# Local attention's scores of two heads as two 64-row matmuls into two PSUM banks

## The chip, the cores and the metric

One Trainium2 chip; the kernel runs on one of its cores. The core has a matrix engine (TensorE, PE in the profile; its weight loads are PEld), VectorE (DVE), ScalarE (ACT), GpSimd (POOL) and a queue engine (SyncE, SP), with an on-chip memory (SBUF) of 128 partitions and an accumulator memory (PSUM) of eight banks, each 512 float32 wide in every partition. The metric is the time of one execution on the device in microseconds, and a kernel's time is the median of its runs.

## The reference

Two layers over 528 tokens (16 learned ones and 512 of the input), width 1024. In each layer a normalized input is projected and split into three mixers: a state-space mixer (S5), local attention with 8 query heads, 2 key heads and a window of 128, and latent attention with 4 heads over all earlier tokens. The three results are normalized, joined, projected and added to the stream; a squared-ReLU MLP of width 4096 follows. What the change touches is the local attention:

```python
qb = q.reshape(bsz, nb, BLOCK, SWA_KV_HEADS, grp, HEAD_DIM)      # BLOCK 128, 2 key heads, grp 4, HEAD_DIM 64
kk, vv = with_prev(kb), with_prev(vb)                            # a block's keys and the block before
s = jnp.einsum('bnqhgd,bnkhd->bnhgqk', qb, kk) * (HEAD_DIM ** -0.5)
s = s - slopes * dist                                            # and -1e30 outside the window
m = jnp.maximum(jnp.max(s, -1, keepdims=True), sink)
p = jnp.exp(s - m)
p = p / (jnp.sum(p, -1, keepdims=True) + jnp.exp(sink - m))
o = jnp.einsum('bnhgqk,bnkhd->bnqhgd', p, vv)
```

All of it is float32.

## The kernel before

The activations are held transposed, features on partitions. The tokens are cut into two halves, A of 272 and B of 256. The large projections go through `gemm` (L182): a weight block of 1024 x 128 is loaded by SP's queue, split into a high part (ScalarE) and a rest (VectorE, L154), and 24 matmuls with 128 x 128 weights go into one PSUM bank "d", of which there are two. In layer 0, half A, the first nine blocks use the exact float32 weights instead (L174); such a float32 matmul leaves two records in the profile, one a pass.

`weave` sets the order: a main stream (projections, output projection, MLP) yields its estimated time after each block, and two side streams, `s5_half` (the state-space mixer of one half) and `attn_half` (both attentions of one half), are advanced by a given share of it. The tile framework then orders each engine's instructions by priority and by what is ready, gives every tile a buffer of its tag, and makes a new user of a buffer wait until the one before it is released.

PSUM's banks are all in use: "d" has two; "bu" two (one tile); "y", "s", "o" and "pt" one each.

`attn_half` goes over units in three steps that are staggered: `first` computes scores and the softmax of a unit, `second` transposes the probabilities of the unit before (L756, into "pt"), `third` multiplies those of the unit before that with the values (L780, into "o"; two heads side by side, each on 64 of the array's 128 columns). A local unit is one block of 128 queries and two query heads, one of each key head: per layer 8 units for each half, so 32. Its two heads are done by one matmul of 128 rows (L697), since the query tile holds head g on partitions 0 to 63 and head g + 4 on 64 to 127. The keys "k2" are stored twice, once for each key head, with zeros on the other's 64 partitions. The scores of both heads stand side by side in the bank "s", 2 x 256 columns, or 2 x 144 for the first block. The softmax reads each head's part with one fused VectorE instruction (L611); ScalarE's exponentials follow. A unit for the 16 learned tokens (L709) exists in layer 0 only.

In `w_in` block 5 yields the keys: VectorE scales the projection into a scratch tile "ch", and ScalarE copies 64 partitions of it into each key head's part of "k2". The zeros come from GpSimd in `open_layer` (L411).

`s5_half` uses PSUM so: the input is spread over 128 partitions for each of two column blocks (L516, bank "y", copied out by ScalarE), projected to states (L530, "bu", read by VectorE in L535 and L536), scanned, projected back (L574, "y", read in L576), and this twice; then comes a gate (L595, "bu", read in L596) and a column sum for the norm (L224, "y"). `startB` opens half B's projections; in layer 1 its column sums use "y". `s5_prep` builds tables and holds one "y" (L351, L365). In the MLP of layer 1 `gemm` uses "bu" for every second pair of halves (L163).

Of the kernel before, what the change touches and what calls it, by code (L numbers as in the profile page):

```python
# [12 lines left out]
F32 = mybir.dt.float32  # L13
# [7 lines left out]
P = 128  # L21
# [3 lines left out]
NM = 16  # L25
# [51 lines left out]
def hybrid(ctx, tc, xT, wblk, small, wglu, wuq, wukv, bD, cD, ident_d, bias_d, tbias_d, mask_d, rope_d, tau_d, outT):  # L77
# [119 lines left out]
    def chain_tmp():  # L197
        return rows(mk(nt, [P, 3, 272], F32, "ch"))
# [12 lines left out]
    def sumsq(tm, src, nk, n):  # L211
# [7 lines left out]
                V.tensor_tensor(acc, acc, sq, op=ALU.add)  # L219
        return acc  # L220

    def colsum(acc, n, tag, second=None):
        ps = mk(psd if tag == "d" else psm, [P, 512], F32, tag)
        PE.matmul(ps[:, :n], lhsT=ones[:, 0:1].to_broadcast([P, P]), rhs=acc, start=True, stop=second is None)  # L224
        if second is not None:
            PE.matmul(ps[:, :n], lhsT=ones[:96, 0:1].to_broadcast([96, P]), rhs=second, start=False, stop=True)
        return ps[:, :n]
# [34 lines left out]
    def s5_prep(L):  # L262
# [85 lines left out]
        nc.gpsimd.memset(tt, 0.0)  # L348
        nci = vt[:, 0, 1]
        V.tensor_scalar(nci, vt[:, CL - 1, 1], -1.0, None, op0=ALU.mult)  # L350
        t3 = mk(psm, [P, 512], F32, "y")  # L351
        cmul(ws[:, :, :, CL - 1], braw, cr, ci)
        yield 2.4
        for m in range(1, CL):
# [48 lines left out]
    def open_layer(L):  # L403
        kv_ = mk(mem, [P, KVW], F32, "kv")
        L["kh"] = kv_[:96, :4 * T].rearrange("p (d t) -> p d t", d=4)
        L["k2"] = kv_[:, 4 * T:6 * T].rearrange("p (d t) -> p d t", d=2)
        L["vm"] = kv_[:, 6 * T:6 * T + 1280].rearrange("p (t c) -> p t c", t=5)
        L["vs"] = mk(mem, [P, 5, P], F32, "vs")
        for kv in range(2):
            o = 64 * (1 - kv)  # L410
            nc.gpsimd.memset(L["k2"][o:o + 64, kv, :], 0.0)  # L411
        nc.gpsimd.memset(L["vm"][:, 0], 0.0)
        nc.gpsimd.memset(L["vs"][:, 0], 0.0)

    def w_in(L, hf, ar, M):
        l, n, t0 = L["l"], HN[hf], H0[hf]
        a, r = ar

        def scaled(out, ps):
            V.tensor_tensor(out, ps, r[:, :out.shape[1]], op=ALU.mult)  # L420
        M["hf"], M["done"] = hf, set()
        M["y"] = mk(mem, [P, KD, 272], F32, f"big{hf}")
        qq = mk_slot(F32)
        M["q"] = qq[:, 0:1088]
        M["qh"] = qq[:, 1088:2176].rearrange("p (d t) -> p d t", d=4)
        M["u"] = qq[:, 2176:2720].rearrange("p (k t) -> p k t", k=2)
        M["cq"] = qq[:, 2720:3264].rearrange("p (k t) -> p k t", k=2)
        M["ckv"] = qq[:, 3264:3536]
        M["v"] = qq[:, 3536:3808]
        M["rope"] = qq[:, 3808:4352].rearrange("p (k t) -> p k t", k=2)  # L430
        nc.gpsimd.dma_start(out=M["rope"][:, :, :n], in_=rope_d[:, :, t0:t0 + n])
        nc.gpsimd.memset(M["cq"][64:96, 1, :n], 0.0)
        for bi, b in enumerate(ORD[hf]):
            if l + hf == 0 and bi == NF:
                a, _ = gains(l, hf, 0, n, "g_in", False)
            ps, = gemm(l, b, [(a, n)])
            if b < 2:
                V.tensor_tensor(M["u"][:, b, :n].rearrange("p (q k) -> p k q", q=CL),
                                ps[:, :n].rearrange("p (k q) -> p k q", q=CL),
                                r[:, :n].rearrange("p (k q) -> p k q", q=CL), op=ALU.mult)  # L440
            elif b == 2:
                scaled(M["ckv"][:, :n], ps[:, :n])
            elif b == 3:
                t = [x[:, :n] for x in chain_tmp()]
                scaled(t[2], ps[:, :n])
                act(M["cq"][0:64, 1, :n], t[2][0:64])
                V.tensor_tensor(t[0][64:96], t[2][64:96], M["rope"][64:96, 0, :n], op=ALU.mult)
                V.tensor_tensor(t[1][96:128], t[2][96:128], M["rope"][96:128, 1, :n], op=ALU.mult)
                act(t[2][64:96], t[1][96:128])
                V.tensor_tensor(t[0][64:96], t[0][64:96], t[2][64:96], op=ALU.add)  # L450
                act(L["kh"][64:96, :, t0:t0 + n], t[0][64:96].unsqueeze(1).to_broadcast([32, 4, n]))
            elif b == 4:
                scaled(M["cq"][:, 0, :n], ps[:, :n])
            elif b == 5:
                t = chain_tmp()
                scaled(t[0][:, :n], ps[:, :n])
                for kv in range(2):
                    p = slice(64 * kv, 64 * kv + 64)
                    act(L["k2"][p, kv, t0:t0 + n], t[0][p, :n])
            elif b < 10:  # L460
                g = b - 6
                qm = M["q"][:, :1024].rearrange("p (t g c) -> p t g c", t=2, g=4)[:, :, g, :]
                c0 = n - 256
                V.tensor_tensor(qm, ps[:, c0:n].rearrange("p (t c) -> p t c", t=2),
                                r[:, c0:n].rearrange("p (t c) -> p t c", t=2), op=ALU.mult)
                if c0 and l < DEPTH - 1:
                    scaled(M["q"][:, 1024 + NM * g:1024 + NM * g + NM], ps[:, :NM])
            else:
                scaled(M["v"][:, :n], ps[:, :n])
            M["done"].add(b)  # L470
            yield cost(l, hf, FULL_IN, n) if bi < NF or l + hf else cost(l, hf, (), n)
# [8 lines left out]
    def finish(L, M, a0, a1, s5):  # L480
        l, hf = L["l"], M["hf"]
        o0, m = span(l, hf)
        y = M["y"]
        if "mixed" not in M:
            M["mixed"] = mk_slot(F32)[:, :2176].rearrange("p (k t) -> p k t", k=KD) if (l, hf) in FULL_OUT else mk_hl()
        mx_ = M["mixed"]
        tm = mix_tmp(s5)
        acc = sumsq(tm, lambda k: y[:, a0 + k, o0:o0 + m], a1 - a0, m)
        r = rsqrt(tm, colsum(acc, m, "y" if s5 else "o"), m, 128 * (a1 - a0))
        yield 1.5  # L490
        for k in range(a0, a1):
            t = y[:, k, o0:o0 + m]
            if (l, hf) in FULL_OUT:
                V.scalar_tensor_tensor(mx_[:, k, :m], t, sm(l, "g_heads", k), r, op0=ALU.mult, op1=ALU.mult)
                yield 0.4
                continue
            V.tensor_tensor(t, t, r, op=ALU.mult)
            split(mx_[:, 0, k, :m], mx_[:, 1, k, :m], t, sm(l, "g_heads", k))
            yield 0.7

    def s5_half(L, M):
# [7 lines left out]
            s5["sv"] = mk(mem, [P, 2, 8], F32, "sv")  # L509
        sv = s5["sv"]  # L510
        u4 = mk(wk, [P, 2, 272], F32, "u3")
        for o in range(2):
            ups = mk(psm, [P, 512], F32, "y")
            for j in range(4):
                for q in range(CL):
                    PE.matmul(ups[32 * q:32 * q + 32, j * K:j * K + K], lhsT=ident[:, 32 * j:32 * j + 32],  # L516
                              rhs=M["u"][:, o, q * K:q * K + K], start=True, stop=True, tile_position=(0, 32 * q))
            act(u4[:, o, :n], ups[:, :n])
# [6 lines left out]
        for o in range(2):  # L525
# [36 lines left out]
            if hf == 0:  # L562
                V.tensor_tensor(sv[:, 0, iq], wv[:, 0, :, K - 1], qv[:, 1, :, K - 1], op=ALU.subtract)
                V.scalar_tensor_tensor(sv[:, 1, iq], qv[:, 0, :, K - 1], -1.0, wv[:, 1, :, K - 1], op0=ALU.mult, op1=ALU.subtract)
            yps = mk(psm, [P, 512], F32, "y")
            for q in range(CL):
                for m in range(3):
                    for j in range(4):
# [52 lines left out]
    def attn_half(L, M):  # L621
# [68 lines left out]
        def first(u):  # L690
            kind, j, o, g = u
            s_ = mk(wk, [P, 544], F32, "s_", bufs=2)
            if kind == "swa":
                ks, nk = (0, NM + P) if j == 1 else (NM + P * (j - 2), 2 * P)
                sp = score()
                c0 = 512 * ((j - 1) % 2) + P * g
                PE.matmul(sp[:, :2 * nk].rearrange("p (e k) -> p e k", e=2), lhsT=M["q"][:, c0:c0 + P],  # L697
                          rhs=L["k2"][:, :, ks:ks + nk], start=True, stop=True)
                s2 = s_[:, :2 * nk + 2].rearrange("p (e k) -> p e k", e=2)
                ns = L["nsink"]  # L700
                nc.gpsimd.tensor_copy(s2[:, :, nk:], ns[:, :8].rearrange("p (e g) -> p e g", e=2)[:, :, g:g + 1])
                vs = [s2[:, e] for e in range(2)]
                softmax([(vs[e], lambda e=e: [(sp[:, nk * e:nk * e + nk], 0, nk)], bias[:, 4 * e + g, 256 - nk:],
                          ns[:, 4 * e + g:4 * e + g + 1]) for e in range(2)], nk, 0.125, True)
                return vs
            if kind == "swah":
                sp = score()
                for e in range(2):
                    PE.matmul(sp[64 * e:64 * e + 64, :NM], lhsT=M["q"][:, 1024:1088], rhs=L["k2"][:, e, 0:NM],  # L709
                              start=True, stop=True, tile_position=(0, 64 * e))  # L710
                nc.gpsimd.tensor_copy(s_[:, NM:NM + 1], L["nsink"][:, 8:9])
                softmax([(s_, lambda: [(sp[:, :NM], 0, NM)], tbias, L["nsink"][:, 8:9])], NM, 0.125, True)
                return [s_]
# [248 lines left out]
    for l in range(DEPTH):  # L962
# [28 lines left out]

        def s2():
            if not winB:
                startB("y")
            s5_ok = 3
            o = obuf(0)
            tm = [mk(nt, [P, 272], F32, "rl", bufs=2) for _ in range(2)]
# [152 lines left out]
```

## Time and profile before

| | |
|---|---|
| median of 3 runs | 1277.2 us (1275.5 to 1279.62) |
| the profiled execution | 1275.43 us |
| its span, first to last instruction | 1273.5 us |
| mean granted clock of TensorE | 0.986 of full speed |
| TensorE busy | 1214.2 us, 95% |
| VectorE busy | 859.1 us, 67% |
| ScalarE busy | 864.9 us, 68% |
| GpSimd busy | 43.3 us, 3% |

How to read the profile: an engine is busy while one of its instructions runs, and an instruction is named by engine and source line, often with "tile written <- tiles read". A PE form such as 128*64 128x128 is rows and columns of the array that are used, then partitions and columns of the output. Matmuls are pipelined, so the durations of neighbours overlap; the distance from one start to the next tells what an instruction takes in a stream. The chain of waits follows the work that ended last back from the end, at each step to what released it.

### The profile page before, as it was taken

The page shows a single profiled execution, that of the slowest core. Times are in us where ns is not written, and L with a number is a line of the kernel's source. Part 1 is how long each engine was busy: PE and PEld are TensorE (multiplying, and loading weights), DVE is VectorE, ACT ScalarE, POOL GpSimd, SP SyncE. Part 2 cuts the span into 40 slices and gives each one's busy share as a digit, 9 for nine tenths or more (in the row PEclk, how much of TensorE's full clock was granted, in tenths as well). Part 3 has the DMA queues.
Part 4 walks back from the last instruction along what each step waited for, and adds up shares of the span by engine and source line. Part 5 has one row for each costly group of instructions (what it writes and reads, how often), then busy time and mean ns, then how long its engine had stood idle before and what let it go on. Part 6 is the DMA issues. An engine that isn't in the chain of part 4 may idle for free.

```text
span 1273.5 us, 27373 instructions
## 1 busy us (share of the span) xinstructions
PE 1214.2 (95%) x10256; PEld 1131.9 (89%) x10256; DVE 859.1 (67%) x1992; ACT 864.9 (68%) x2012; POOL 43.3 (3%) x103
## 2 busy tenths in 40 slices
PE   6999998999999999899999988999999999999985
PEld 4788886899999999888899987778999999999985
DVE  7888768869755657856776789766684343334775
ACT  6787787997764657766786776798675632534764
POOL 4000002000000000000000000000000000000000
PEclk9999998999999999999999989999989999999998
DMA  6233423254665556433345642324646333334652
GB/s 227 76 100 101 136 66 100 78 166 130 196 181 175 175 175 206 118 123 112 105 150 174 193 141 83 100 76 125 185 145 178 95 96 91 92 101 128 187 185 90
DMA packets 93236, 170.55 MB, mean 134 GB/s; under 512 B 10960, under 2 KB 14032, under 8 KB 93104
## 3 DMA queue, kind: packets, MB, share of 16 engines
q1 hardware_dynamic: 90288, 161.62, 41.7%
q0 software_dynamic: 2816, 7.18, 1.8%
q8 instruction: 81, 1.33, 0.4%
q14 instruction: 51, 0.42, 0.1%
HBM read 166.66 MB, written 2.10 MB: 133 GB/s over the span
## 4 chain that ended last, share of the span: by engine, by line
PE 45%; DVE 4%; ACT 3%; DMA 1%; issue 1%; DVEq 0%; ACTq 0%
PE d L182 32%; PE bu L182 7%; PE o L780 1%; DMA raw<-in_wblk 1%; PE pt L756 1%; PE s L697 1%; DVE big L810 1%; ACT w L133 1%; ACT slot L133 1%; DVE w L154 1%; DVE h L811 1%; PE s L732 1%; ACT ch L133 1%; PE o L224 0%; ACT rl L133 0%
## 5 line engine op out<-in xcount | busy, mean ns | idle before, releaser
L182 PE MATMUL d<-slot,w 128*128 128x256 f32 (+1 forms) x6936 | 911.8, 289 | 20.6 <-ACT slot L133 5.6
L182 PEld LDWEIGHTS d<-slot,w 128*128 128x128 f32 x6936 | 861.7, 190 | 48.9 <-issue 13.9
L154 DVE TENSOR_TENSOR w<-raw,w 128x512 fp32r<-128x512 f32 x578 | 396.9, 691 | 214.3 <-ACT w L133 204.7
L133 ACT ACTIVATE w<-raw 128x512 fp32r<-128x512 f32 x578 | 360.3, 627 | 233.8 <-PE d L182 168.4
L189 DVE TENSOR_TENSOR slot<-rl,slot 128x256 fp32r<-128x256 f32 (+1 forms) x128 | 54.2, 428 | 60.4 <-ACT slot L133 58.2
L182 PE MATMUL bu<-slot,w 128*128 128x256 f32 x768 | 92.9, 280 | 0.0
L182 PEld LDWEIGHTS bu<-slot,w 128*128 128x128 f32 x768 | 91.4, 188 | 0.0
L133 ACT ACTIVATE rl<-d 128x256 f32<-128x256 f32 (+1 forms) x144 | 54.2, 376 | 33.6 <-PE d L182 31.9
L133 ACT ACTIVATE slot<-rl 128x256 fp32r<-128x256 f32 (+1 forms) x128 | 52.6, 419 | 2.6
L133 ACT ACTIVATE rl<-rl 128x256 f32<-128x256 f32 (+1 forms) x128 | 52.6, 418 | 1.9
L174 PE MATMUL d<-slot,raw 128*128 128x272 f32 x144 | 38.5, 413 | 10.6 <-DMA raw<-in_wblk 10.6
L885 DVE TENSOR_TENSOR big<-d,big 128x256 f32<-128x256 f32 (+1 forms) x80 | 34.2, 428 | 15.5 <-PE d L182 12.3
L174 PEld LDWEIGHTS d<-slot,raw 128*128 128x128 f32 x144 | 28.1, 200 | 17.5 <-ACT ch L133 10.6
L133 ACT ACTIVATE ph<-pt 128x512 f32<-128x512 f32 (+2 forms) x66 | 36.4, 552 | 6.4 <-PE pt L756 6.0
L219 DVE TENSOR_TENSOR ch<-ch 128x256 f32<-128x256 f32 (+1 forms) x84 | 35.8, 426 | 5.9 <-ACT ch L133 5.9
L133 ACT ACTIVATE slot<-h,small 128x256 fp32r<-128x256 f32 (+2 forms) x72 | 32.0, 504 | 9.2 <-DVE h L811 4.9
L697 PE MATMUL s<-kv,slot 128*128 128x512 f32 (+1 forms) x64 | 31.5, 574 | 1.5 <-ACT vs L133 0.7
L133 ACT ACTIVATE ch<-h 128x256 f32<-128x256 f32 (+1 forms) x64 | 25.3, 413 | 7.5 <-DVE ch L219 6.6
L192 DVE SCALAR_TENSOR_TENSOR slot<-h,small,slot 128x256 fp32r<-128x256 f32 (+1 forms) x64 | 27.7, 484 | 1.0 <-ACT slot L133 1.0
L732 PE MATMUL s<-kv,slot 96*128 96x264 f32 (+3 forms) x80 | 26.3, 410 | 0.5 <-DVE nm L611 0.4
L780 PE MATMUL o<-ph,vs 128*64 128x128 f32 x256 | 22.7, 286 | 0.0
L810 DVE TENSOR_TENSOR big<-big,ch 128x512 f32<-128x512 f32 (+1 forms) x32 | 21.0, 693 | 0.1
(651 smaller groups left out, 1133.9 us busy)
## 6 DMA issues: line engine op xcount, KB each, us to landing
raw<-in_wblk SPq DMA_DIRECT2D x600, 256.0 KB, 2.7
ph<-in_wuq POOLq DMA_DIRECT2D x8, 256.0 KB, 3.1
h<-in_xT SPq DMA_DIRECT2D x4, 272.0 KB, 4.2
h<-in_xT SPq DMA_DIRECT2D x1, 1024.0 KB, 10.5
ph<-in_wukv POOLq DMA_DIRECT2D x4, 256.0 KB, 3.4
u<-in_wglu POOLq DMA_DIRECT2D x4, 256.0 KB, 3.7
out<-h SPq DMA_DIRECT2D x1, 1024.0 KB, 5.7
out<-h SPq DMA_DIRECT2D x4, 256.0 KB, 2.3
```

Source lines behind the costliest of these rows:

```text
L133: S.activation(out, in_, func, **kw)
L154: V.tensor_tensor(w[:, 1].rearrange("p k m -> p (k m)"), raw, f32(hi), op=ALU.subtract)
L174: PE.matmul(ps[:, :n], lhsT=raw[:, k * P:(k + 1) * P], rhs=a[:, 4 * q + k, :n], start=q + k == 0, stop=q + k == 4)
L182: PE.matmul(ps[:, :n], lhsT=w[:, wi, k, :], rhs=a[:, ai, 4 * q + k, :n], start=i == 0, stop=i == 23)
L189: V.tensor_tensor(lo, src, f32(hi), op=ALU.subtract)
L192: V.scalar_tensor_tensor(lo, src, gain, f32(hi), op0=ALU.mult, op1=ALU.subtract)
L219: V.tensor_tensor(acc, acc, sq, op=ALU.add)
L697: PE.matmul(sp[:, :2 * nk].rearrange("p (e k) -> p e k", e=2), lhsT=M["q"][:, c0:c0 + P], rhs=L["k2"][:, :, ks:ks + nk], start=True, stop= ...
L732: PE.matmul(sp, lhsT=M["qh"][0:96, 2 * g + e, o:o + P], rhs=L["kh"][:, 2 * g + e, c0:c1], start=True, stop=True)
L780: PE.matmul(ops[64 * e:64 * e + 64, :P], lhsT=v, rhs=pp[:, P * e:P * e + P], start=i == 0, stop=i == len(ph) - 1, tile_position=(0, 64 * e))
L810: V.tensor_tensor(x, x, rb, op=ALU.mult)
L885: V.tensor_tensor(ac[:, b, :n], ps[:, :n], ac[:, b, :n], op=ALU.add)
```

## The change

Each head's scores become a matmul of their own on 64 rows: head e uses partitions 64e to 64e + 63 of queries and keys, is put on that row half of the array, and writes to a bank of its own ("s" and a new "s2"). The keys need no zero halves: "kt" holds both key heads on their partitions, and block 5 scales straight into it; scratch tile, copies and the memsets for "k2" go. The learned tokens' unit uses 64 rows and 64 columns for each head. The bank for "s2" is freed by removing "y": its users take a tile of the two banks "bu", the two spreads of `s5_half` one bank of a common tile each, the others the first bank.

```diff
+    def two_banks():
+        return mk(psm, [P, 2, 512], F32, "bu")
+
     def colsum(acc, n, tag, second=None):
-        ps = mk(psd if tag == "d" else psm, [P, 512], F32, tag)
+        ps = two_banks()[:, 0] if tag == "bu" else mk(psd if tag == "d" else psm, [P, 512], F32, tag)
...
-        t3 = mk(psm, [P, 512], F32, "y")
+        t3 = two_banks()[:, 0]
...
-        L["k2"] = kv_[:, 4 * T:6 * T].rearrange("p (d t) -> p d t", d=2)
+        L["kt"] = kv_[:, 4 * T:5 * T]
...
-        for kv in range(2):
-            o = 64 * (1 - kv)
-            nc.gpsimd.memset(L["k2"][o:o + 64, kv, :], 0.0)
...
             elif b == 5:
-                t = chain_tmp()
-                scaled(t[0][:, :n], ps[:, :n])
-                for kv in range(2):
-                    p = slice(64 * kv, 64 * kv + 64)
-                    act(L["k2"][p, kv, t0:t0 + n], t[0][p, :n])
+                scaled(L["kt"][:, t0:t0 + n], ps[:, :n])
...
-        r = rsqrt(tm, colsum(acc, m, "y" if s5 else "o"), m, 128 * (a1 - a0))
+        r = rsqrt(tm, colsum(acc, m, "bu" if s5 else "o"), m, 128 * (a1 - a0))
...
+        both = two_banks()
         for o in range(2):
-            ups = mk(psm, [P, 512], F32, "y")
+            ups = both[:, o]
...
-            yps = mk(psm, [P, 512], F32, "y")
+            yps = two_banks()[:, 0]
...
-                sp = score()
+                sp = [score(), mk(psm, [P, 512], F32, "s2")]
                 c0 = 512 * ((j - 1) % 2) + P * g
-                PE.matmul(sp[:, :2 * nk].rearrange("p (e k) -> p e k", e=2), lhsT=M["q"][:, c0:c0 + P],
-                          rhs=L["k2"][:, :, ks:ks + nk], start=True, stop=True)
+                for e in range(2):
+                    p = slice(64 * e, 64 * e + 64)
+                    PE.matmul(sp[e][:, :nk], lhsT=M["q"][p, c0:c0 + P], rhs=L["kt"][p, ks:ks + nk], start=True, stop=True,
+                              tile_position=(64 * e, 0))
...
-                softmax([(vs[e], lambda e=e: [(sp[:, nk * e:nk * e + nk], 0, nk)], bias[:, 4 * e + g, 256 - nk:],
+                softmax([(vs[e], lambda e=e: [(sp[e][:, :nk], 0, nk)], bias[:, 4 * e + g, 256 - nk:],
...
-                    PE.matmul(sp[64 * e:64 * e + 64, :NM], lhsT=M["q"][:, 1024:1088], rhs=L["k2"][:, e, 0:NM],
-                              start=True, stop=True, tile_position=(0, 64 * e))
+                    p = slice(64 * e, 64 * e + 64)
+                    PE.matmul(sp[p, :NM], lhsT=M["q"][p, 1024:1088], rhs=L["kt"][p, 0:NM],
+                              start=True, stop=True, tile_position=(64 * e, 64 * e))
...
-                startB("y")
+                startB("bu")
```

## Rows read from the trace of the kernel before

**Rows 1.** The page: busy us, share of the span and instructions.
```profile
PE 1214.2 (95%) x10256; PEld 1131.9 (89%) x10256; DVE 859.1 (67%) x1992; ACT 864.9 (68%) x2012; POOL 43.3 (3%) x103
```

**Rows 2.** Stretch, length, busy us of PE, PEld, DVE, ACT, POOL; clock, DMA share, GB/s.
```profile
50.00:75.00 25.00, 23.82 (x144) 17.07 (x143) 20.70 (x88) 23.03 (x71) 2.84 (x8) 1.00 0.32 96
163.00:178.00 15.00, 14.94 (x121) 10.29 (x122) 6.75 (x30) 12.19 (x39) 0.75 (x4) 1.00 0.11 32
569.00:620.00 51.00, 50.39 (x605) 44.53 (x604) 36.78 (x101) 30.98 (x81) 3.27 (x7) 1.00 0.36 109
813.00:840.00 27.00, 26.51 (x180) 19.21 (x178) 18.63 (x62) 25.87 (x74) 1.44 (x6) 1.00 0.17 51
...
770.00:792.00 22.00, 18.50 (x272) 17.03 (x271) 21.70 (x52) 12.81 (x30) 0.00 (x0) 0.92 0.20 60
```

**Rows 3.** The chain of waits near 573 and 822 us: start, us, what.
```profile
572.59 0.86 PE s L697 x2
...
573.99 0.13 PE d L182
574.12 0.40 PE pt L756 x3
...
577.16 0.48 PE s L697 x2
...
821.53 0.59 PE o L780 x8
822.12 1.05 PE s L697 x2
```

**Rows 4.** PE in order of time, 108 to 110 us: start, us, instructions.
```profile
108.09 0.66 PE L780 MATMUL o<-ph,kv 128*64 128x128 f32 x8
108.68 1.10 PE L182 MATMUL d<-slot,w 128*128 128x256 f32 x7
109.71 0.66 PE L780 MATMUL o<-ph,kv 128*64 128x128 f32 x8
```

**Rows 5.** The chain of waits in the MLP of layer 1.
```profile
992.86 5.64 PE bu L182 x48
```

**Rows 6.** PE in order of time: the first and the last of 32 local units.
```profile
50.64 0.75 PE L697 MATMUL s<-kv,slot 128*128 128x288 f32 x2
...
838.48 1.02 PE L697 MATMUL s<-kv,slot 128*128 128x512 f32 x2
```

**Rows 7.** In order of time: state-space halves 1 and 4, by engine.
```profile
98.17 0.49 DVE L576 SCALAR_TENSOR_TENSOR big<-slot,small,y 128x272 f32<-128x272 f32 x1
98.77 0.78 PE L530 MATMUL bu<-u,wt 128*128 128x68 f32 x6
...
771.55 2.00 PE L530 MATMUL bu<-u,wt 128*128 128x64 f32 x16
773.36 2.60 PE L182 MATMUL d<-slot,w 128*128 128x256 f32 x20
779.15 1.01 PE L516 MATMUL y<-slot,ident 128*32 128x64 f32 x32 [3.19 <-DVE slot L438]
...
779.18 0.68 DVE L535 TENSOR_TENSOR wP<-bu,tab 128x512 f32<-128x512 f32 x1
...
780.54 0.37 ACT L133 ACTIVATE u<-y 128x256 f32<-128x256 f32 x1
```

**Rows 8.** Who waited for whom on PE: us in total, times, longest.
```profile
PE d L174 <- DMA raw<-in_wblk: 10.6, 1, 10.6
...
PE y L516 <- ACT u L133: 0.8, 1, 0.8
...
PE s L697 <- DVE nm L611: 0.6, 2, 0.4
```

**Rows 9.** Instructions that write or read tile kv: duration ns, first to last start.
```profile
L133 ACT ACTIVATE kv<-ch x12: 405/428/1112, 27.5 to 800.8; 64x272 f32<-64x272 f32 x4, 64x256 f32<-64x256 f32 x4, 32x1088 f32<-32x1088 f32 x2, 32x1024 f32<-32x1024 f32 x2
L411 POOL MEMSET kv<- x4: 532/534/537, 5.2 to 513.8; 64x528 f32 x4
```

## The prediction

> **What bounds the kernel now.** I read the page first: TensorE (PE) is busy 95% of 1273.5 us, VectorE and ScalarE two thirds [rows 1]. The profiled execution took 1275.43 us, 1.9 more than its span; the median of the runs, 1277.2, stands 0.14% above it. The table by stage then says whether PE is the bound where the change works. The local scores run in four stretches, and PE is busy 95, 99.6, 98.8 and 98.2% of them [rows 2]. In the last of them ScalarE is nearly as full: it has 27 - 25.87 = 1.1 us to spare, and what PE saves beyond that ScalarE holds back. The chain of waits agrees: around 573 and 822 us it runs along PE, through scores (L697), projection matmuls (L182), transposes (L756) and value products (L780) [rows 3].
>
> **The scores, priced.** A float32 matmul leaves two records, one a pass. Of the 32 local units 24 stream 512 columns a pass and 8, those of the first block, stream 288. In the chain a unit of 512 takes 0.86 us between full-array neighbours, 0.43 a pass; one of 288 takes 0.48. Behind a value product (L780), whose matmuls fill half of the array's columns, the same 512 take 1.05 [rows 3]. These 0.2 us are the price of changing how the array is divided, and a second view says so. Eight L780 records from 108.09 us take 0.59 us until the next instruction; the seven L182 behind them take 1.03 until L780 returns [rows 4]. In a long run 48 of L182 take 5.64 us [rows 5], 0.1175 each, so seven are 0.82 and 0.21 is on top. The eight L780 passes of 128 columns would take 0.86 one by one (0.43 x 128/512 = 0.107 each); two at a time they take 0.43, and 0.16 is on top. So column halves run side by side, and each change of division costs 0.16 to 0.21 us: the array runs empty, then the next weights load uncovered.
>
> The Trainium skill (TensorEngine Tiling (Array Packing), Key Properties) says that a switch of the tiling mode drains TensorE, while different tiles work in parallel. Both halves of that agree with the rows just read. Its section Theoretical Speedup gives up to 2x for a contraction of 64: by that alone the scores would take 12.2 us less, with the drain at the traced price only 2.6.
>
> No row shows two row halves of the array. The nearest is the column pair, and I take its behaviour: both heads' passes side by side, a unit of 512 streaming 2 x 0.215 = 0.43 us and one of 288 streaming 0.24. Each unit then has an entry and an exit of 0.21 us, the price with 128 columns of weights. I sorted the units by what stands beside them on PE, from the first at 50.64 us to the last at 838.48 [rows 6]:
> - 9 of 512 between full-array work, no wait: 0.86 becomes 0.43 + 0.42 = 0.85, together -0.1 us.
> - 14 of 512 that pay for one change now, or whose weights load uncovered behind a wait: 1.07 becomes 0.85, 14 x -0.22 = -3.1.
> - 1 of 512, at 163 us, inside a group of quarter-column matmuls, which pays twice now: -0.4.
> - 6 of 288 between full-array work: 0.48 becomes 0.24 + 0.42 = 0.66, 6 x 0.18 = +1.1.
> - 2 of 288 behind a wait: -0.1 together.
>
> The sum is -2.6 us, of which 1.5 fall in the last stretch (seven units at -0.22); there I count the 1.1 that ScalarE has to spare. That leaves -2.2. Bounds: if row halves cost no change, 24 x 0.43 + 8 x 0.24 = 12.2 us go; if the heads do not overlap at all, this 12.2 is not saved while the changes are paid, 12.2 - 2.6 = +9.6. The head-block unit (L709, 16 columns) is divided before and after: 0.
>
> **The banks.** The new bank "s2" is taken from "y", whose users move into "bu". Two chains of buffers become one: spread of u, bu, y product, bu, y product, gate, column sum, each waiting until the one before it is read. The second bu now waits for the y product's reader (L576). In the tightest of the first three halves that reader ends at 98.66 us and bu begins at 98.77 anyway [rows 7]: 0. In the last half the second bu stands ahead of that reader today and moves behind it; PE idles 3.5 of 22 us around there [rows 2] and can take it in: 0, at most its own 1.8.
>
> Two things do change. The two spreads of u get a bank each, so the 0.82 us that PE waits for ScalarE's copy at 140 us [rows 8] go: -0.8; in the other halves other work fills that place. And in the last half the first bu stands at 771.55, right behind the first spread and long before the second, which has 3.19 us of PE idle before it, waiting for VectorE (L438) [rows 7]. With one pair of banks bu can't begin before the second spread's copy ends at 780.91. Its time, until the next matmul, is 773.36 - 771.55 = 1.8 us; it leaves a place where PE would otherwise idle and comes where PE has work: +1.8. What is late next is VectorE's reading of bu (L535, 779.18 now, some 783 then), but VectorE has other work without a gap there (21.70 of 22 us, [rows 2]) and only changes its order. Bounds 0 and 3.8, the delay of L535.
>
> **Two banks, two releases.** Each head's score waits for its own bank, so other work can slip between the heads. Such cuts exist: at 574 us an L182 stands between the first transpose of a unit and its other three [rows 3]. A cut pair takes two passes of 0.215 twice and four changes, 0.86 + 0.84 against 0.85: +0.85 us. It threatens where a score waits for the softmax that reads the bank: two places [rows 8]. I take one: +0.8; bounds 0 and 1.7.
>
> **Keys.** Eight copies on ScalarE (0.42 us each, four key blocks) and four memsets of 0.53 on GpSimd go [rows 9]. ScalarE's copies lie behind PE's stream in three of the four blocks; in the fourth, the last half, PE has idle time, and two copies, 0.8 us, could come back. But the last of them starts at 800.8 [rows 9], 12 us before that half's scores, so I take 0. GpSimd's queue starts its small DMAs 1.1 us earlier; the first matmul waits 10.6 us for a weight DMA of SP's queue [rows 8]: 0. Without that cover it would be 1.1.
>
> **Sum.** -2.2 - 0.8 + 1.8 + 0.8 = -0.4 us: 1275.0 beside the profiled 1275.4, and 1276.8 on the median. About 0.3%, 3.8 us, is what a measurement of this kernel tells from no change; so I forecast no difference.
>
> **Rivals.**
> - *Row halves switch for next to nothing.* For it: part of the traced price is weight loading (0.16 with narrow weights, 0.21 with wide ones), and row halves load separate rows. Against it: every group with divided columns that I read pays. With the scores at -5 to -12.2 the sum is -3 to -10: 1267 to 1274. Chance 0.22, faster. (The Trainium skill's 2x, in TensorEngine Tiling (Array Packing), Theoretical Speedup, is this case at its best.)
> - *Row halves do not run side by side.* For it: no row shows them. In full the sum is 9.6 + 1.8 - 0.8 = +10.6, 1288; if each head's second pass goes ahead of the other head's first, three pass times stand for two, +6.1, and the sum is near +5, 1282. It decides once the second head's first pass starts 0.2 us behind the first head's in all units. Chance 0.14, slower.
> - *The shared banks hold up the state-space half.* For it: seven uses in one chain, on a full VectorE. Against it: the gaps read above, and attention, not this half, ends each layer's mixing. With L535's 3.8 us on the path and a wait of 1 to 2 us in two other halves: 1280 to 1284. Chance 0.10, slower.
> - *Cut pairs.* Ten of 32 cut cost 8.5 us: 1284. Chance 0.04, slower.
>
> **How the numbers follow.** The likeliest case, price and gain of the division near cancelling, has 0.50 and its own range of 1273 to 1281. The cases together reach from 1267 to 1288; the serial case in full and the free switch at its best, some 0.12 together, are left out: 1268 to 1285. Faster 0.22, same 0.50, slower 0.28.
>
> **What the profile after should show.** Twice as many L697 records, on 64 rows, the heads' passes starting within 0.02 us of each other; a unit between two L182 at 0.85 us as before, one behind L780 0.2 shorter, one of 288 0.2 longer. The 0.82 us wait for ScalarE gone. PE's wait for L438 near 779 at 5 us, with bu behind it. L182's 5.64 per 48 unchanged, ScalarE 3.4 us less busy. I am wrong if the heads run one after the other, if the instruction behind a unit starts without the 0.2 us, or if PE gets new waits for L536 or L576.

## The result: slower by 1%, outside the range

The changed kernel takes 1291.5 us in the median of its runs (1286.0 to 1292.2), beside 1276.5 for the kernel before on the same chip: 1.0104 times as long, with a 95% interval of 1.0086 to 1.0122. The ratio is taken over all runs and not from the medians, which lie 15 us apart. By it the loss is some 13 us, where 0 was forecast and 1285 was the upper end. The profiled execution took 1290.98 us, its span is 1289.2.

First the page of the changed kernel, busy time by engine, which answers to [rows 1]; then three groups of its instructions (line, engine, names, shapes, count, busy us, mean ns, idle ahead). The second pair in a shape, 64x256 for the scores, is partitions and columns of the operand that streams in, not of the output, which has 128 partitions here.
```profile
PE 1228.8 (95%) x10320; PEld 1141.0 (89%) x10320; DVE 857.9 (67%) x1992; ACT 859.6 (67%) x2001; POOL 40.9 (3%) x99
```
```profile
L696 PE MATMUL s<-kv,slot 64*128 64x256 f32 (+1 forms) x128 | 30.6, 408 | 1.4 <-DVE slot L460 0.7 <-ACT vs L133 0.4 <-DVE nm L608 0.2
L780 PE MATMUL o<-ph,vs 128*64 128x128 f32 x256 | 24.9, 287 | 0.0
L527 PE MATMUL bu<-u,wt 128*128 128x64 f32 (+1 forms) x128 | 17.0, 290 | 0.1
```
TensorE is not idler than before (60.4 us of the span against 59.3); it is busy 14.6 us longer. So nearly all of the time went into TensorE's work, instructions that take longer, and 1.1 us into more waiting. The scores have twice as many records, as they should. L696 was L697 in the kernel before, L527 was L530, L513 L516 and L571 L574.

The work by stage, as in [rows 2], the stretches moved along with the later kernel:
```profile
50.00:75.00 25.00, 25.00 (x156) 17.75 (x157) 20.86 (x86) 22.80 (x69) 3.21 (x8) 1.00 0.28 80
165.00:180.00 15.00, 14.81 (x141) 9.41 (x140) 5.82 (x30) 12.12 (x38) 0.75 (x4) 1.00 0.07 19
577.00:628.00 51.00, 50.41 (x621) 44.42 (x619) 36.47 (x104) 32.03 (x82) 1.83 (x7) 1.00 0.38 108
825.00:852.00 27.00, 26.47 (x179) 19.34 (x180) 18.31 (x60) 23.74 (x68) 1.60 (x6) 1.00 0.18 49
...
778.00:801.00 23.00, 17.59 (x186) 16.27 (x188) 20.47 (x48) 13.16 (x31) 0.00 (x0) 0.78 0.23 69
```
The four stretches with scores look much as before. The one with the spreads does not: the granted clock is 0.78 over 23 us, and was 0.92 over 22.

**Whole pairs behave as priced.** TensorE in order of time, a unit of 288 columns and one of 512 in the third half:
```profile
577.60 0.52 PE L696 MATMUL s<-kv,slot 64*128 64x144 f32 x4 [0.40 <-ACT vs L133]
578.04 2.65 PE L182 MATMUL d<-slot,w 128*128 128x272 f32 x19
580.63 0.70 PE L696 MATMUL s<-kv,slot 64*128 64x256 f32 x4
581.26 0.66 PE L756 MATMUL pt<-ident,s__1146_7279 128*128 128x128 f32 x4
```
All four passes of the two heads and one change of division fit between 580.63 and 581.26, 0.63 us; streamed one after the other they would need 0.86 without any change. So the row halves run side by side. The 19 matmuls between the units, of 272 columns, take 2.59 us; at the pace of [rows 5], where 256 columns take 0.1175, it would be 19 x 0.125 = 2.37, and the 0.22 on top holds a part of the change from either unit. So a unit of 512 costs 0.63 and some 0.2, which is the forecast 0.85.

**But many pairs are cut.** The second half of layer 0, in order of time:
```profile
142.06 0.70 PE L696 MATMUL s<-kv,slot 64*128 64x256 f32 x2
142.69 0.63 PE L513 MATMUL bu<-slot,ident 128*32 128x64 f32 x26
...
154.31 0.70 PE L696 MATMUL s<-kv,slot 64*128 64x256 f32 x2
154.94 1.39 PE L182 MATMUL d<-slot,w 128*128 128x272 f32 x9
...
164.75 0.70 PE L696 MATMUL s<-kv,slot 64*128 64x256 f32 x2
165.38 0.37 PE L571 MATMUL bu<-wP,vt 128*32 128x64 f32 x11
```
One head alone (two passes) takes 0.63 us to the next instruction, exactly as long as a whole pair. In the order of TensorE's instructions 14 of the 32 pairs are cut in this way: 4 and 6 in the halves of layer 0, 2 and 2 in layer 1. (The trace has 26 heads alone and, at 166 us, two heads that start 0.4 us apart, where those of a whole pair start 0.007 apart.) I had taken one.

**The last state-space half.** The spreads (L513) and the first bu (L527) in order of time, and the waits that answer to the first of [rows 7]:
```profile
778.52 0.65 PE L513 MATMUL bu<-slot,ident 128*32 128x64 f32 x32
779.11 3.09 PE L182 MATMUL d<-slot,w 128*128 128x256 f32 x24
787.29 1.08 PE L513 MATMUL bu<-slot,ident 128*32 128x64 f32 x32 [5.09 <-DVE slot L438]
788.30 1.01 PE L182 MATMUL d<-slot,w 128*128 128x256 f32 x3
789.11 3.51 PE L527 MATMUL bu<-u,wt 128*128 128x64 f32 x16
792.38 3.27 PE L182 MATMUL d<-slot,w 128*128 128x256 f32 x18
```
The wait for L438 is 5.09 us, forecast at 5. But bu behind it takes 3.27 us to the next instruction, and took 1.8. The table by stage in steps of 2 us (length, busy us of TensorE, granted clock, DMA share, GB/s) says why; first the kernel before, then the changed one.
```profile
778.00:780.00 2.00, 0.85 (x32) 0.82 0.00 0
780.00:782.00 2.00, 2.00 (x20) 0.50 0.00 0
782.00:784.00 2.00, 2.00 (x16) 0.83 0.05 12
```
```profile
784.00:786.00 2.00, 0.00 (x0) 0.54 0.00 0
786.00:788.00 2.00, 0.71 (x28) 0.50 0.00 0
788.00:790.00 2.00, 2.00 (x23) 0.50 0.13 31
790.00:792.00 2.00, 2.00 (x12) 0.50 0.62 190
792.00:794.00 2.00, 2.00 (x10) 0.50 0.49 184
794.00:796.00 2.00, 2.00 (x22) 0.90 0.00 0
```
A clock of 0.5 is the lower of TensorE's two levels, 1.2 GHz. From the shares, the kernel before spends 0.7 + 2 + 0.7 = 3.4 us at it behind its idle of 3.19 us. The changed kernel spends 1.8 + 8 + 0.4 = 10.2 us at it; some 7.1 of them come after the wait, when TensorE works. Half of such a stretch is lost if TensorE is what holds up the work: 1.7 us before, 3.6 now. With the 1.9 by which the wait grew, I estimate this one place at 3.8 us.

### The profile page after: what moved, and what is told of

The parts are those of the page before. It is cut to its first block, busy times and chain, and to the rows that moved or that the text cites. A ratio compares the mean times of both kernels' runs of the same rounds, so it can differ in the third digit from the quotient of the medians.

```text
span 1289.2 us, 27496 instructions
## 1 busy us (share of the span) xinstructions
PE 1228.8 (95%) x10320; PEld 1141.0 (89%) x10320; DVE 857.9 (67%) x1992; ACT 859.6 (67%) x2001; POOL 40.9 (3%) x99
## 4 chain that ended last, share of the span: by engine, by line
PE 76%; DVE 9%; ACT 7%; DMA 5%; issue 2%; SPq 0%; DVEq 0%; ACTq 0%
PE d L182 52%; PE bu L182 7%; DMA raw<-in_wblk 5%; PE o L780 3%; PE d L174 2%; PE pt L756 2%; PE s L696 2%; ACT w L133 2%; DVE w L154 2%; PE s L659 1%; DVE big L810 1%; PE s L732 1%; PE bu L527 1%; ACT slot L133 1%; DVE h L811 1%
## 5 line engine op out<-in xcount | busy, mean ns | idle before, releaser
L189 DVE TENSOR_TENSOR slot<-rl,slot 128x256 fp32r<-128x256 f32 (+1 forms) x128 | 54.1, 428 | 60.4 <-ACT slot L133 58.3
L696 PE MATMUL s<-kv,slot 64*128 64x256 f32 (+1 forms) x128 | 30.6, 408 | 1.4 <-DVE slot L460 0.7
L732 PE MATMUL s<-kv,slot 96*128 96x264 f32 (+3 forms) x80 | 26.7, 415 | 1.9 <-DVE nm L608 1.3
L696 PEld LDWEIGHTS s<-kv,slot 64*128 64x128 f32 x128 | 14.2, 188 | 9.7 <-issue 3.1
```

The costliest lines, as they stand in the source:

```text
L189: V.tensor_tensor(lo, src, f32(hi), op=ALU.subtract)
L696: PE.matmul(sp[e][:, :nk], lhsT=M["q"][p, c0:c0 + P], rhs=L["kt"][p, ks:ks + nk], start=True, stop=True, tile_position=(64 * e, 0))
L732: PE.matmul(sp, lhsT=M["qh"][0:96, 2 * g + e, o:o + P], rhs=L["kh"][:, 2 * g + e, c0:c1], start=True, stop=True)
```

## The experiments

All times below are ratios to the kernel before, run beside it on the same chip; 0.001 is 1.28 us. The groups of experiments ran on different chips, so a difference between two groups is one between two such ratios.

**One tile for both heads, and the banks alone.** Two theories stood after the result. Theory A: the cut pairs are the loss. Theory B: the state-space half's merged banks are. Three kernels tell them apart. The first gives both heads' banks to one tile, so that they are taken and released together; all other users of "s" use its first bank:
```
-                sp = [score(), mk(psm, [P, 512], F32, "s2")]
+                both = score()        # mk(psm, [P, 2, 512], F32, "s")
+                sp = [both[:, 0], both[:, 1]]
```


> The two scores of a unit keep their row halves and their two banks, but the banks are one tile, so both heads wait for the same release and stand next to each other on TensorE. Theory A (cut pairs: the second head's bank has no other user, its score is issued apart from the first head's, and each head then pays for its own change of division and overlaps with nothing; 14 of 32 units in the list of instructions): 14 x 0.85 = 12 us come back, 1277 to 1281, and every unit shows two pairs of passes 0.007 us apart. Theory B (the shared banks hold up the state-space half): they are shared as before, so 1287 to 1292.

The second is the kernel before with "y" moved into the pair "bu", and nothing else; scores and keys are the old ones:
```
+        both = two_banks()            # mk(psm, [P, 2, 512], F32, "bu")
         for o in range(2):
-            ups = mk(psm, [P, 512], F32, "y")
+            ups = both[:, o]
...
-            yps = mk(psm, [P, 512], F32, "y")
+            yps = two_banks()[:, 0]
```


> Only the banks are merged (no y, its users in bu); scores, keys and copies are those of the kernel before, and a bank stays unused. Theory A: the merge costs 0 to 3 us, 1276 to 1280. Theory B: most of the 14 us, 1286 to 1291.

The third adds to the second two matmuls on all 128 rows (keys with zero halves) in place of the one, into "s" and "s2": the array is never divided by rows, but the pairs can be cut.
```
-                PE.matmul(sp[:, :2 * nk].rearrange("p (e k) -> p e k", e=2), lhsT=M["q"][:, c0:c0 + P],
-                          rhs=L["k2"][:, :, ks:ks + nk], start=True, stop=True)
+                for e in range(2):
+                    PE.matmul(sp[e][:, :nk], lhsT=M["q"][:, c0:c0 + P], rhs=L["k2"][:, e, ks:ks + nk], start=True, stop=True)
```


> Banks merged, and each head a matmul of its own into its own bank, but on all 128 rows with the zero halves, so the array is never divided; the cuts stand at the same places as in the changed kernel. Theory A: a cut costs nothing without a change of division; two matmuls of half the columns stream as long as one, so about as the banks alone, 1277 to 1282. Theory C (it is the order itself, heads issued early ahead of more urgent work, that costs): as slow as the changed kernel, 1286 to 1292.

Measured: 1.0068 [1.0056, 1.0081] with one tile, 1.0056 [1.0041, 1.0070] with the banks alone, 1.0068 [1.0056, 1.0081] with two full-row matmuls. Both theories hold in part. One tile gives back 4.6 us, where 12 were expected, though 31 of its 32 pairs are whole in the trace. The merged banks cost 7.1 us with the old scores untouched, over half of the loss. The cuts cost the difference between the changed kernel and the one-tile kernel, the same 4.6 us. Cutting alone is cheap: over the banks alone the full-row kernel, with 22 heads alone in its trace, loses 1.5 us (between -0.9 and 4.0), and its trace has 10.2 us at the lower clock in the last half against 6.8. So the cuts seem dear because each half also changes the division; between these two differences alone the intervals still overlap. In the one-tile kernel the 128 records of the scores are busy for 8.9 us less than the changed kernel's:
```profile
L697 PE MATMUL s<-kv,slot 64*128 64x256 f32 (+1 forms) x128 | 21.7, 404 | 1.6 <-ACT vs L133 0.7 <-DVE slot L460 0.7 <-DVE nm L608 0.2
```
Joined scores on top of the banks (first against second kernel) bring no gain, +1.5 us (between -0.9 and 4.0).

**Which part of the banks.** The first of two kernels is the banks alone with a bank for the spreads again; the second, further down, is the kernel before with only the spreads moved.
```
         for o in range(2):
-            ups = both[:, o]
+            ups = mk(psm, [P, 512], F32, "y")
```


> Scores and keys as in the kernel before; y product, column sums and transposes of the set-up share the pair of banks with bu, but the two spreads of u keep a bank of their own, so that the first bu of the last half can run between the spreads again. Theory 1 (the first bu, pushed behind the second spread, is the loss of the merged banks in the last half): of the 6.8 us that the merged banks cost by themselves some 3.5 to 5 come back, the step at 770 to 785 us is gone, TensorE's wait for L438 is 3.2 us again: 1277 to 1279. Theory 2 (the y product and the second bu in one chain are the loss): the time stays at 1281 to 1283. If the spreads' 0.8 us wait at 140 us comes back, it is visible there alone.

The second:
```
+        both = mk(psm, [P, 2, 512], F32, "bu")
         for o in range(2):
-            ups = mk(psm, [P, 512], F32, "y")
+            ups = both[:, o]
```


> The kernel before with one thing moved: the two spreads of u take the pair of banks of bu, a bank each, as in the changed kernel; all else of the state-space half stays in bank y. Theory 1: the first bu of the last half is pushed behind the second spread, TensorE's wait there is 5.1 us, bu takes 3.5 us in place of 2.0, and the kernel loses 3.5 to 5 us: 1278 to 1280. Theory 2: within 1.5 us of the kernel before.

Measured: 1.0026 [1.0014, 1.0037] and 1.0035 [1.0020, 1.0051]. Giving the spreads their bank takes 3.8 us off the 7.1; moving the spreads alone costs 4.5. The two agree: Theory 1 holds for the larger part of the banks' price, and 3.3 us stay with the spreads out of the way. With their own bank the wait for L438 is 3.19 us again, bu takes 1.8 and stands between the spreads, and the stretch at the lower clock is 3.4 us, all as in the kernel before. The trace of the spreads-only kernel shows the step in the forecast place:
```profile
779.90 1.08 PE L517 MATMUL bu<-slot,ident 128*32 128x64 f32 x32 [4.75 <-DVE slot L438]
780.91 1.01 PE L182 MATMUL d<-slot,w 128*128 128x256 f32 x3
781.72 3.51 PE L531 MATMUL bu<-u,wt 128*128 128x64 f32 x16
```
From 780 to 790 us its granted clock is 0.50 in every 2 us. With the shares beside it that is 10.2 us, of which half, 5.1, is lost, 3.4 more than before; the wait is 1.6 longer. The sum of 5.0 stands beside the measured 4.5.

**Is it the clock?** If so, work that nobody reads, put where TensorE idles, should give time back although it adds work. To the banks alone:
```
         for o in range(2):
             ups = both[:, o]
+            if l == DEPTH - 1 and hf == 1 and o == 1:
+                fill = mk(psm, [P, 512], F32, "y")
+                for _ in range(12):
+                    PE.matmul(fill[:, :n], lhsT=ident, rhs=u4[:, 0, :n], start=True, stop=True)
```


> As the kernel with the merged banks alone (1281.8), with 12 matmuls of identity weights by 256 columns, some 5 us of work that nobody reads, put into the last half between the first and the second spread, where TensorE idles 5.1 us. If the clock behind that idle is what makes bu take 3.5 us in place of 2.0: the idle shrinks to under 1 us, the granted clock there stays at full level, bu takes 2.0, and the time is 1279.5 to 1281, in spite of the added work. If the idle is not the cause: bu stays at 3.5 and the time is 1282 or more.

Measured: 1.0032 [1.0021, 1.0044] against 1.0056: 3.1 us less (between 0.7 and 5.4), with 5.4 us of work added. In the traces the time from the first spread to the first key product of the latent attention (L638 in the kernel before) falls from 25.0 to 22.8 us. The same fill in the one-tile kernel, written into the second spread's own bank (twelve `PE.matmul(ups[:, :n], lhsT=ident, rhs=u4[:, 0, :n], start=True, stop=True)`):

> Both heads' scores in one tile of two banks, merged banks, all as in the one-tile kernel, and 12 matmuls that nobody reads (identity weights, 256 columns, some 5 us) into the second spread's own bank, ahead of that spread, where TensorE idles 5.1 us. If what is lost in the last half is TensorE's clock behind the idle: bu takes 2.0 us in place of 3.5, and of the 8.3 us that the one-tile kernel loses 3 to 5 come back: 1.0025 to 1.0045 times the kernel before. If the clock is not the cause there: 1.006 or more.

Measured: 1.0007 [0.9998, 1.0015] against 1.0068. That is 7.8 us, more than the 3 to 5 that the theory had for it. TensorE in order of time in this kernel:
```profile
771.86 5.44 PE L513 MATMUL bu<-u,ident 128*128 128x256 f32 x24
776.95 2.12 PE L182 MATMUL d<-slot,w 128*128 128x256 f32 x15
779.45 0.65 PE L516 MATMUL bu<-slot,ident 128*32 128x64 f32 x32 [0.38 <-DVE slot L438]
780.03 0.74 PE L182 MATMUL d<-slot,w 128*128 128x256 f32 x4
780.61 2.00 PE L530 MATMUL bu<-u,wt 128*128 128x64 f32 x16
782.42 2.35 PE L182 MATMUL d<-slot,w 128*128 128x256 f32 x18
```
The idle of 5.09 us is 0.38, bu is back at 2.00, and the granted clock is 1.00 in every 2 us from 776 to 790. The clock is shown as a cause: the same stretch, from the first spread to the first key product, takes 22.8 us in place of 26.2. That is 3.4 of the 7.8. The two profiles lie 9.1 us apart; besides the 3.4 they show 0.9 ahead of the spreads, 2.5 in the attention and the projections behind, 1.5 in the MLP, whose stream is slower in the one-tile profile (last section), and 0.8 after it. What the fill has to do with those parts is open.

The same twelve lines in the changed kernel itself, cuts and all:

> The changed kernel as it is, with its two tiles for the scores and 14 of 32 pairs cut, and the same 12 matmuls that nobody reads ahead of the second spread of the last half. Theory: the cuts cost their own time on TensorE, 4.6 us by the medians and 6.4 by the profiles (changed kernel against one-tile kernel), whatever the clock does in the last half; the fill gives back 3 to 7 us: 1.0040 to 1.0060 times the kernel before, 4 to 6 us above the one-tile kernel with the fill (1.0007). Rival: what the cut pairs lost was TensorE's clock in the last half too, and with the fill both kernels end alike, at 1.0020 or less.

Measured: 1.0086 [1.0067, 1.0105], above both expectations. The fill gives back 2.3 us here, not clear of noise (between -1.0 and 5.6), though the granted clock is 1.00 in every 2 us from 776 to 800. The rival is out: the cuts keep their price with the clock up. Between this kernel and the one-tile kernel with the fill that price is 10.1 us, between the same two without it 4.6; the intervals (7.4 to 12.8 and 1.8 to 7.4) just touch, so by the runs I hold it at 5 to 10. The traces put it at about 7 both times. The first long group of the MLP starts, by the chain of waits (start, us, what), in the kernel before, the changed and the one-tile kernel, and then in the latter two with the fill, at:
```profile
981.58 5.64 PE bu L182 x48
995.95 5.68 PE bu L182 x48
989.22 5.68 PE bu L182 x48
989.50 5.68 PE bu L182 x48
982.42 5.64 PE bu L182 x48
```
That is 6.7 us between the two without the fill and 7.1 with it, each from one execution.

**The kernel before, filled.** Its own idle there is 3.2 us, and three others are longer than 3.5. First the same loop with `range(7)` into the second spread's bank:

> The kernel before and nothing of the change, with 7 such matmuls (3.0 us) into the second spread's own bank, where TensorE idles 3.2 us. In the kernel before, TensorE runs at half clock for some 3.3 us behind this idle. If the clock is the cause: that stretch goes and 1 to 2 us are gained, 0.9985 to 0.9992 times the kernel before. If not: the time stays or grows by up to 0.5 us.

Then also the other three, in the matmul helper, at the three blocks that stand behind these idles:
```
+            if uid[0] in (438, 1054, 1523):
+                spare = pss[0] if uid[0] == 438 else psm.tile([P, 512], F32, tag="pt", name=f"spare_{uid[0]}")
+                for _ in range(17):
+                    PE.matmul(spare[:, :P], lhsT=ident, rhs=ident, start=True, stop=True)
```


> As the kernel before with 7 matmuls in the idle ahead of the second spread, and 17 matmuls of identity by 128 columns (3.6 us) in each of the three other long idles of TensorE (3.8 us at 198, 4.2 at 518, 3.9 at 745 us), into a bank that is free there. Behind each of these TensorE runs at half clock for some 6 us. If an idle of TensorE costs its own length and then half of that stretch: some 3 us come back at each, 9 to 11 in all, about 1266 to 1268. If the clock falls anyway, or the filling work delays what is behind it: 1274 or more.

Measured: 1.0011 [0.9999, 1.0022] and 0.9997 [0.9986, 1.0009], no change both times, where 1 to 2 us and 9 to 11 were expected. The theory as I had written it is too simple. At the four places TensorE spends 20.4 us at the lower level in the kernel before (6.8, 3.4, 6.8 and 3.4) and 3.4 with four fills; half of the difference would be 8.5 us, and the time does not follow. With one fill the stretch from the first spread to the first key product takes 21.9 us at full clock and took 22.0 before, so TensorE does not set its length there, and what it won goes into waits such as the next one, for ScalarE, 0.5 us in the kernel before (L638 there):
```profile
PE s L641 <- ACT kv L133: 1.5, 1, 1.5
```
So a stretch at the lower level costs its half only where TensorE is the bound behind it. In the merged kernels it is for a good part of it, by the 2.2 and 3.4 us above.

**Spreads in another bank.** A way to have joined scores and an early first bu: the spreads in the transposes' bank "pt", in the one-tile kernel.
```
-            ups = both[:, o]
+            ups = mk(psm, [P, 512], F32, "pt")
```


> The changed kernel with both heads' scores in one tile of two banks, and the two spreads of u in the bank of the attention's transposes, pt, in place of the pair of bu. Theory 1: the first bu stands between the spreads again and 3.5 to 6 of the 8.3 us that the one-tile kernel loses come back: 1277.5 to 1280. Rival: the spreads hold up the transposes or wait for them, and the time is 1283 or more.

Measured: 1.0066 [1.0050, 1.0083], no gain over 1.0068. The wait for L438 is 3.2 us again and bu takes 2.0, as Theory 1 wanted; the time is lost elsewhere, as the rival had it: beside the kernel before, its trace reaches the same projection matmuls 1.0 us early near 225 us and 9.1 late near 268. Its mean clock is the lowest of all these profiles, 0.978.

**Keys.** The one-tile kernel with the old keys:
```
-                scaled(L["kt"][:, t0:t0 + n], ps[:, :n])
+                t = chain_tmp()
+                scaled(t[0][:, :n], ps[:, :n])
+                for kv in range(2):
+                    p = slice(64 * kv, 64 * kv + 64)
+                    act(L["k2"][p, kv, t0:t0 + n], t[0][p, :n])
...
```


> The one-tile kernel with the keys as before: two tiles with zero halves, their four memsets and the two copies for each key block are back, and the 64-row matmuls read the half of the rows that is not zero. The keys part was forecast to bring nothing: the time is that of the one-tile kernel, 1.0068, within 1 us. Rival: ScalarE's copies lie on the path in the last half, and the time is 1 to 2 us longer than the one-tile kernel's.

Measured: 1.0059 [1.0046, 1.0072] against 1.0068. The intervals overlap: no effect of the keys is seen, as forecast.

## Why the prediction failed, by its steps

**The scores, priced: right, and worth as much as forecast once TensorE's clock is up.** A whole pair costs what was worked out. With the fill in both kernels, joined scores and their keys against the old ones on merged banks are 1.0007 against 1.0032, -3.2 us (between -1.4 and -5.0), where -2.2 was forecast; in the two traces the MLP's first long group starts at 982.42 and 985.67, 3.3 apart. Without the fill the same comparison gives +1.5; the one-tile kernel spends 10.2 us at the lower clock around the spreads, the banks alone 6.8, and from the first spread to the first key product it takes 26.2 us against 25.0. That is 1.2 of it; the rest is within the noise. The rival that row halves do not overlap is out, and so is the one that they switch for nothing.

**Two banks, two releases: the step that failed first.** I asked where a score waits for the softmax that reads its bank, and found two places. The question was wrong. What matters is who else uses each bank. "s" also holds the kp, qp and vt products of the attention (L635, L659, L672) and the latent attention's scores (L732); "s2" has no other user. So the second head's score can go as soon as queries and keys are there, while the first head's stands behind those products. That is how I read the heads sent alone at 142 and 154 us, amid the L635 and L659 products, long before their partners; the one-tile kernel, where 31 pairs are whole, bears it out. Fourteen pairs at the forecast 0.85 us would be 11.9, in place of the 0.8 in the sum; measured are 5 to 10, and 7 by the traces. The rival of ten cut pairs had a chance of 0.04, which is where the error of judgement lies.

**The banks: the move right, the price too small.** The first bu moved behind the second spread, and the wait grew to 5.09 us, both as written. What I took as the price, bu's own 1.8 us, left out that TensorE works at half clock for longer behind a longer idle. The spreads alone cost 4.5 us (between 2.6 and 6.5) and all merged banks 7.1 (between 5.2 and 8.9), above the upper bound of 3.8, which I had set by L535's delay, another mechanism. In [rows 2] the clock of that stretch stood at 0.92; I read past it. The Trainium skill (TensorE: Matmul & The Clock Gate, HAM oscillation — how this bites in real kernels) describes the same pattern for waits on DMA: a long enough wait drops the array to half rate and the next work starts slow. The trace agrees here for a wait on VectorE, 0.50 behind 5.09 us.

**The second bu and the rest of the chain: "0, at most its own 1.8" was too small as well.** With the spreads in a bank of their own 3.3 us of the banks' price stay. One reading of it was that the state-space half ends later and its pieces fall among the attention's. In the banks-only kernel the gate's product (L599) runs from 829.66 us among the value products, which come in pieces there, each with its changes of division:
```profile
829.66 1.13 PE L599 MATMUL bu<-wP,u 128*128 128x256 f32 x4
830.73 0.43 PE L784 MATMUL o<-ph,vs 128*64 128x128 f32 x2
```
The value products on tile vs are busy 23.8 us in that kernel, 22.7 in the kernel before. But with the spreads in their own bank, where the 3.3 us stay, they are at 22.7 again:
```profile
L783 PE MATMUL o<-ph,vs 128*64 128x128 f32 x256 | 22.7, 286 | 0.0
```
So this reading does not explain the 3.3 us. In that kernel's one trace the same projection matmul comes 1.8 us later than in the kernel before already near 268 us, and the MLP's first long group 2.0 later; the spreads-only trace is 0.2 late at the former. So in that trace the loss does not come from the last half, and which step of the chain causes it stays open.

**The gain of 0.8 us from a bank for each spread was not there.** The banks-only kernel still has the wait of [rows 8], with both spreads on banks of their own:
```profile
140.44 0.65 PE L520 MATMUL bu<-slot,ident 128*32 128x64 f32 x32 [0.82 <-ACT u L133]
```
In the changed kernel other work stands between the two spreads, one lone head among it, and the wait is gone from the list.

**The sum.** By the runs without a fill: banks +7.1, joined scores with their keys +1.5, cuts +4.6, together 13.2; the whole is 13.3. That they add up is no test, since each is a difference between neighbours. With the fill the same path is +4.1, -3.2 and +10.1, 11.0 in all. So the sizes of the last two terms are known only roughly: the interval of each is 2 to 3 us either way. Banks and cuts were each a rival, with one in seven between them; that both would happen was no case of mine, and the range ended below it.

No version here beats the kernel before. The best with joined scores, one tile and the fill, is level with it at 1.0007. The Trainium skill (TensorEngine Tiling (Array Packing), Gotcha 1: PSUM Pressure) warns that row tiles need a bank each; here that bank, taken from the state-space half, cost more than the row halves brought.

## What to carry to other kernels

Before two halves of an operation get two banks, list every other user of each bank: if the lists differ, the halves will be scheduled apart, and where each half changes the array's division the whole gain goes. Give them one tile. When a buffer is merged into another chain, price not only the work that moves but the idle that it leaves: on a TensorE that is the bound, a wait of 5 us was followed by 7 to 10 us at the lower clock, up to half of which is lost, and a dozen matmuls that nobody reads bought a part of it back. Where TensorE was not the bound behind the idle, in the kernel before, they bought nothing.

## What the runs showed of the hardware

The stretches at the lower clock level do not simply follow the wait ahead of them. Behind 3.19 us of idle the kernel before spent 3.4 us at it. Behind 5.09 us the banks-only kernel spent 6.8 (a last share of 0.93, three of 0.50, one of 0.87 in steps of 2 us):
```profile
780.00:782.00 2.00, 0.45 (x22) 0.93 0.00 0
782.00:784.00 2.00, 2.00 (x28) 0.50 0.00 0
784.00:786.00 2.00, 2.00 (x12) 0.50 0.77 220
786.00:788.00 2.00, 2.00 (x11) 0.50 0.51 181
788.00:790.00 2.00, 2.00 (x22) 0.87 0.00 0
```
The one-tile and the changed kernel, with the same wait, spent 10.2. In the changed kernel some 3.1 of them lie still in the wait. What decides between 6.8 and 10.2 no run here shows. A long idle is not needed either: in the kernel with four fills TensorE is busy with a fill from 198.5 us, goes on with four matmuls, waits 1.40 us for VectorE, and then spends 3.4 us at the lower level (clock 0.62 and 0.53 in the two steps from 206 us).

In the MLP of layer 1 the profiled changed kernel has a slightly slower stream than [rows 5], 5.68 us for 48 matmuls instead of 5.64, at full clock. Over this stretch that adds some 1.5 us to its profile. The profiles of the one-tile kernel, of the banks alone with the fill and of the changed kernel with the fill have it too; the other ten have 5.64, the banks alone and the one-tile kernel with the fill among them. So it goes neither with the scores nor with the banks. With one profile of each kernel no run shows whether it belongs to an execution or to a kernel; if to a kernel, it is some 1.5 us of each difference above between one that has it and one that has not.
